# Remainders of the first layer's memory weights: made by adding DMAs onto the negated weights

## The chip, the cores and the metric

The kernel runs on one core of a Trainium2 chip. The metric is device time in microseconds for one execution of the whole program; the median of the runs is quoted. A profiled execution gives the durations used below.

## What is computed

A two-layer encoder over 512 tokens of width 1024. Each layer runs a token mixer (latent attention in the first layer, grouped-query attention in the second) beside a 4-head cross-attention into 256 memory tokens, merges both in one output projection, and then applies a SwiGLU block. The part that the change touches is the projection of the memory tokens into keys and values:

```python
def _memory_attention(q, mem_n, w_kv, q_norm, k_norm):
    q = _rmsnorm(q.reshape(B, S, MEM_HEADS, MEM_HEAD_DIM), q_norm)
    kv = (mem_n @ w_kv).reshape(B, M, 2, MEM_HEADS, MEM_HEAD_DIM)
    k = _rmsnorm(kv[:, :, 0], k_norm)
    v = kv[:, :, 1]
    s = jnp.einsum('bqhd,bmhd->bhqm', q, k)
    p = jax.nn.softmax(s * (MEM_HEAD_DIM ** -0.5), axis=-1)
    return jnp.einsum('bhqm,bmhd->bqhd', p, v).reshape(B, S, MEM_W)

mem_n = _rmsnorm(mem, mem_norm)
for i in range(DEPTH):
    ...
    mem_out = _memory_attention(q_mem, mem_n, w_mem_kv[i], memq_norm[i], memk_norm[i])
```

`w_kv` is 1024 x 1024 for each layer, so `mem_n @ w_kv` is 256 x 1024 x 1024.

## The kernel before

Every matrix product is taken in three passes (`mm3`, L137 to L139). Each fp32 operand is split into a leading part `hi`, its value rounded to the matmul's fp32r format, and a remainder `lo`, the value less `hi`, rounded the same way. The product is hi\*hi, hi\*lo and lo\*hi, summed in PSUM. A weight chunk goes through `load_w`: SyncE loads it from HBM into a tile `raw` (L170), ScalarE casts it into `whi` (L158), and VectorE subtracts to get `wlo` (L159).

The memory part (`mem_part`) of a layer is two halves, keys (c = 0) and values (c = 1), of eight chunks of 128 x 512 each: 16 chunks per layer. Each chunk is multiplied with two blocks of 128 memory tokens, so six matmuls of 512 columns per chunk; the first, third, fourth and sixth of them need only `whi`, the second and fifth need `wlo`. The PSUM banks of the first layer are named `mm_173` and `mm_174` (keys) and, for the values, `mm_264` and `mm_265`. The memory tokens themselves (`memT`) are scaled by gains into `g` tiles by ScalarE (L247) and VectorE (L250), and squared on ScalarE (L261).

In the first layer the memory part is one of four streams that `merge` writes out interleaved: attention units, the projections of queries and keys by head group (banks `sc`, later `mm`), the memory stages, and the start of the output projection. From what is written, the framework's scheduler fixes the order on each engine, with latencies of its own for each operation. Each engine then runs its list strictly in order, and waits on semaphores where a tile is not ready. POOL (GpSimd) issues a few loads of rotary tables at the start and then nothing until the first feed-forward block, where it issues DMAs that add a weight block in HBM onto a block in SBUF (L815, L947, L981). All other loads are issued by SyncE.

The weight pool holds 7 `raw`, 6 `whi` and 6 `wlo` tiles at this stage. A tile is reused once its readers are done.

Of the kernel before, what the change touches and what calls it, by code (L numbers as in the profile page):

```python
# [12 lines left out]
F32R = mybir.dt.float32r  # L13
I32 = mybir.dt.int32
AF = mybir.ActivationFunctionType
ALU = mybir.AluOpType
# [32 lines left out]
def encoder_kernel(ctx: ExitStack, tc: tile.TileContext, a: dict, out: bass.AP):  # L49
    nc = tc.nc  # L50
    V, A, PE, GP = nc.vector, nc.scalar, nc.tensor, nc.gpsimd
# [12 lines left out]
    def wtile(dt, tag, bufs=None):  # L64
        return wpool[0][1].tile([P, wpool[0][2]], dt, tag=tag, name=nm(tag), **({"bufs": bufs} if bufs else {}))
# [6 lines left out]
    def nm(s):  # L72
        uid[0] += 1
        return f"{s}_{uid[0]}"

    def g4(shape=(P, 1024), dt=F32R, name="g"):
        return gp_.tile(list(shape), dt, tag="G", name=nm(name))

    def pair(dt=F32R, n=512, name="g"):

        t = g4((P, 2, 512), dt, name)
        return t[:, 0, :n], t[:, 1, :n]
# [3 lines left out]
    def gt(shape=(P, 512), dt=F32R, kind=""):  # L86

        h = halves.pop((dt, kind), None)
        if h is None:
            h, halves[dt, kind] = pair(dt)  # L90
        if len(shape) == 2:
            return h[:, : shape[1]]
        if len(shape) == 3:
            return h.rearrange("p (a b) -> p a b", a=shape[1])
        return h.rearrange("p (a b c) -> p a b c", a=shape[1], b=shape[2])
# [7 lines left out]
    def bank(tag):  # L103
        return ps.tile([P, 512], F32, tag=tag, name=nm(tag), bufs=CFG[tag])
# [4 lines left out]
    def f(ap):  # L109
        return ap.bitcast(F32)  # L110
# [20 lines left out]
    def gcol(i):  # L131
        return gains[:, i : i + 1]


    def mm3(out, lh, rh, start, stop, skip=False):
        (lhi, llo), (rhi, rlo) = lh, rh
        PE.matmul(out, lhi, rhi, start=start, stop=False, skip_group_check=skip)  # L137
        PE.matmul(out, lhi, rlo, start=False, stop=False, skip_group_check=skip)  # L138
        PE.matmul(out, llo, rhi, start=False, stop=stop, skip_group_check=skip)  # L139
# [3 lines left out]
    def eng(kind):  # L143
        c = cnt.get(kind, 0)
        cnt[kind] = c + 1
        p = CFG[kind]
        return p[c % len(p)]

    phase = ["s"]

    def wsplit(raw, n, kind, neg=False):

        hi, lo = wtile(F32R, "whi"), wtile(F32R, "wlo")
        if neg:
            A.mul(hi[:, :n], raw, -1.0)
            V.scalar_tensor_tensor(lo[:, :n], raw, -1.0, f(hi[:, :n]), ALU.mult, ALU.subtract)
            return hi, lo
        A.copy(hi[:, :n], raw)  # L158
        (V if eng(kind) == "V" else GP).tensor_sub(lo[:, :n], raw, f(hi[:, :n]))  # L159
        return hi, lo  # L160
# [3 lines left out]
    def load_raw(src, n):  # L164
        if wpool[0][2] == 1024:
            nraw[0] += 1
            raw = wtile(F32, "raw", CFG["RF"]) if nraw[0] % 2 and CFG["RF"] else g4(dt=F32, name="raw")
        else:
            raw = wtile(F32, "raw", CFG["W"])
        nc.sync.dma_start(raw[:, :n], src)  # L170
        return raw

    def load_w(src, n):
        return wsplit(load_raw(src, n)[:, :n], n, "wlo" + phase[0])

    def w_units(src, unit):

        n = src.shape[1] // unit
        per = max(1, wpool[0][2] // unit)
        nch = -(-n // per)  # L180
        u = 0
        for c in range(nch):
            m = (n - u + nch - c - 1) // (nch - c)
            w = load_w(src[:, u * unit : (u + m) * unit], m * unit)
            for j in range(m):
                yield wcols(w, j * unit, (j + 1) * unit)
            u += m

    def wcols(w, a0, a1):
        return w[0][:, a0:a1], w[1][:, a0:a1]  # L190
# [54 lines left out]
    def split_gain(dst, src, g):  # L245
        if eng("hi") == "A":
            A.mul(dst[0], src, g)  # L247
        else:
            V.tensor_scalar_mul(dst[0], src, g)
        V.scalar_tensor_tensor(dst[1], src, g, f(dst[0]), ALU.mult, ALU.subtract)  # L250
# [5 lines left out]
    def acc_sq(acc, src, first):  # L256
        if first:
            A.activation(acc, src, AF.Square)
        else:
            s = tt()  # L260
            A.activation(s[:, : acc.shape[1]], src, AF.Square)  # L261
            V.tensor_add(acc, acc, s[:, : acc.shape[1]])
# [60 lines left out]
    def tsl(x, t):  # L323
        return x[0][:, t * P : (t + 1) * P], x[1][:, t * P : (t + 1) * P]
# [11 lines left out]
    def k_outer(outs, acts, src, ncols, tags, pre=()):  # L336

        outs += [bank(tg)[:, :ncols] for tg in tags]
        nk = len(acts)
        rest = w_units(src[:, len(pre) * ncols :], ncols)  # L340
        for k in range(nk):
            w = pre[k] if k < len(pre) else next(rest)
            for t in range(4):
                mm3(outs[t], tsl(acts[k], t), w, k == 0, k == nk - 1)
            yield 12 * ncols / 2370
# [247 lines left out]
    def mem_part(l, c, outs, hm):  # L593

        outs += [bank("mm"), bank("mm")]
        m = None
        per = CFG["WC"] // NM
        for k, w in enumerate(w_units(a["w_mkv"][l, c], 512)):
            if c == 0:
                if k % per == 0:  # L600
                    n = min(per, NK - k) * NM
                    m = load_raw(a["memT"][:, k * NM : k * NM + n], n)
                h = gt((P, 2, NM), kind="m")
                h = (h[:, 0], h[:, 1])
                split_gain(h, m[:, (k % per) * NM : (k % per + 1) * NM], gcol(G_MEM + k))
                hm.append(h)
                if l == 0:
                    if k == 0:
                        acc_m.append(gt(dt=F32)[:, :NM])
                    acc_sq(acc_m[0], m[:, (k % per) * NM : (k % per + 1) * NM], k == 0)  # L610
            h = hm[k]
            for t in range(2):
                mm3(outs[t], tsl(h, t), w, k == 0, k == NK - 1)
            yield 1.3

    def mem_stages(l, kts, vts):
        xs, ssqs, hm = [], [], []

        def k_head():
            outs = []  # L620
            yield from mem_part(l, 0, outs, hm)
            xs.extend(raw_copy(o, 512) for o in outs)
            ssq = small(8, "ssqm")
            for t in range(2):
                head_ssq(ssq[:, 4 * t : 4 * t + 4], [xs[t]], 4, P)
            ssqs.append(ssq)
# [21 lines left out]
        def v_head():  # L648
            outs = []
            yield from mem_part(l, 1, outs, hm)  # L650
            for t in range(2):
                v = pair()
                split_gain(v, outs[t], r_mem[0][:, t : t + 1])
                vts.append(v)
# [12 lines left out]
    def out_prefix(l, acts, banks, pre, n, tag, ready):  # L667


        while not ready():  # L670
            yield None
        banks += [bank(tag) for _ in range(n)]
        for kp in range(3):
            yield from out_block(banks, range(n), acts, kp, list(w_units(a["w_out"][l, 0, kp], 512)), kp == 0, False)
        pre.append(w_early(a["w_out"][l, 0, 3], 2))
        while (l, 7) not in fin:
            yield None
        weight_pool(True)
        pre.append(list(w_units(a["w_out"][l, 0, 4], 512)))
# [436 lines left out]
    for o in range(5):  # L1116
        c = pair()
# [475 lines left out]
```

## Time and profile before

| what | us |
|---|---|
| median of 3 runs | 1249.2 |
| lowest and highest run | 1248.47, 1249.56 |
| the profiled execution's own time | 1250.35 |
| its span, first to last instruction | 1248.2 |
| TensorE busy in the span | 1234.2 (99%) |
| VectorE busy | 996.7 (80%) |
| ScalarE busy | 754.4 (60%) |
| POOL busy | 63.5 (5%) |

The profiled execution took 1.15 us more than the median. Its span leaves out 2.15 us around the first and the last instruction. A matmul of 512 columns is shown with some 380 to 400 ns, but the next one starts about 227 ns after it: matmuls overlap in the array, so gaps under about 0.15 us between two of them don't show as idle time and are seen only in their starts.

### The profile page before, as it was taken

To read this page: it belongs to the slowest core of one execution; us is meant where nothing else is said; L and a number is where in the kernel's file an instruction comes from. 1 tells how busy PE (TensorE), PEld (TensorE's weight loads), DVE (VectorE), ACT (ScalarE), POOL (GpSimd) and SP (SyncE) were. 2 spreads that over 40 slices of the span, in tenths; PEclk is the share of its full clock that TensorE was granted. 3 is DMA by queue.
4 is the path that set the end of the run, shared out by engine and by line. 5 is a ranking of instruction groups with operands and counts; after the bars stand their busy time and mean duration, and the time that the engine had idled before them with its cause. 6 is when DMAs were issued, how large, how long until landed. Compare 5 with 4: busy or idle time off the path is not lost.

```text
span 1248.2 us, 17265 instructions
## 1 busy us (share of the span) xinstructions
PE 1234.2 (99%) x6305; PEld 1037.6 (83%) x6305; DVE 996.7 (80%) x1778; ACT 754.4 (60%) x1293; POOL 63.5 (5%) x83
## 2 busy tenths in 40 slices
PE   9999999999999999999999999999999999999998
PEld 6988878888778888888888888888887888889887
DVE  6699999854888877899857797976388977789984
ACT  6597776754755555577453578867375555556742
POOL 1000000001000000021100000000000000002110
PEclk9999999999999999999999999999999999999999
DMA  7342101055274344695733211323436344459681
GB/s 235 118 149 81 35 9 68 1 202 167 56 216 118 112 132 112 220 244 156 156 110 101 86 51 60 110 69 119 143 77 194 100 140 140 119 171 253 158 178 67
DMA packets 54964, 157.05 MB, mean 126 GB/s; under 512 B 6320, under 2 KB 10928, under 8 KB 54880
## 3 DMA queue, kind: packets, MB, share of 16 engines
q1 hardware_dynamic: 44784, 119.58, 27.7%
q0 software_dynamic: 10096, 36.38, 15.4%
q8 instruction: 49, 0.80, 0.3%
q14 instruction: 35, 0.29, 0.1%
HBM read 153.84 MB, written 2.10 MB: 125 GB/s over the span
## 4 chain that ended last, share of the span: by engine, by line
PE 94%; DVE 3%; ACT 2%; DMA 1%; issue 0%; SPq 0%
PE mm L138 15%; PE mm L139 14%; PE mm L137 14%; PE sc L138 12%; PE sc L137 12%; PE sc L139 12%; PE tp L351 6%; PE sc L504 4%; DVE wlo L159 1%; PE tp L137 1%; PE tp L139 1%; PE tp L138 1%; ACT whi L158 1%; PE tp L570 1%; DMA raw<-in_w_cin 1%; ACT t L902 0%
## 5 line engine op out<-in xcount | busy, mean ns | idle before, releaser
L158 ACT CAST whi<-raw 128x1024 fp32r<-128x1024 f32 (+3 forms) x370 | 330.5, 898 | 310.9 <-PE sc L139 199.9
L159 DVE TENSOR_TENSOR wlo<-raw,whi 128x1024 fp32r<-128x1024 f32 (+3 forms) x370 | 378.6, 1028 | 156.6 <-ACT whi L158 153.7
L138 PE MATMUL mm<-wlo,op 128*128 128x512 f32 (+1 forms) x456 | 172.7, 379 | 3.3 <-DVE wlo L159 3.3
L137 PE MATMUL mm<-whi,op 128*128 128x512 f32 (+1 forms) x456 | 173.0, 379 | 0.3 <-ACT whi L158 0.2
L139 PE MATMUL mm<-whi,op 128*128 128x512 f32 (+1 forms) x456 | 171.9, 377 | 0.0
L139 PE MATMUL sc<-whi,op 128*128 128x512 f32 (+1 forms) x456 | 171.6, 376 | 0.0
L138 PE MATMUL sc<-wlo,op 128*128 128x512 f32 (+1 forms) x456 | 171.6, 376 | 0.0
L137 PE MATMUL sc<-whi,op 128*128 128x512 f32 (+1 forms) x456 | 171.5, 376 | 0.0
L137 PE MATMUL mm<-whi,g 128*128 128x512 f32 (+3 forms) x370 | 141.3, 383 | 0.0
L138 PE MATMUL mm<-wlo,g 128*128 128x512 f32 (+3 forms) x370 | 139.1, 376 | 0.0
L139 PE MATMUL mm<-whi,g 128*128 128x512 f32 (+3 forms) x370 | 138.2, 376 | 0.0
L138 PEld LDWEIGHTS mm<-wlo,op 128*128 128x128 f32 x456 | 85.9, 188 | 20.9 <-DVE wlo L159 5.9
L137 PEld LDWEIGHTS mm<-whi,op 128*128 128x128 f32 x456 | 85.9, 188 | 15.9 <-ACT whi L158 0.8
L138 PEld LDWEIGHTS sc<-wlo,op 128*128 128x128 f32 x456 | 85.8, 188 | 15.7
L139 PEld LDWEIGHTS sc<-whi,op 128*128 128x128 f32 x456 | 85.8, 188 | 15.6
L137 PEld LDWEIGHTS sc<-whi,op 128*128 128x128 f32 x456 | 85.8, 188 | 15.5
L139 PEld LDWEIGHTS mm<-whi,op 128*128 128x128 f32 x456 | 85.9, 188 | 15.3
L137 PEld LDWEIGHTS mm<-whi,g 128*128 128x128 f32 x370 | 69.6, 188 | 10.5 <-ACT g L247 0.7
L139 PEld LDWEIGHTS mm<-whi,g 128*128 128x128 f32 x370 | 69.4, 188 | 10.5 <-DVE g L250 0.2
L138 PEld LDWEIGHTS mm<-wlo,g 128*128 128x128 f32 x370 | 69.7, 188 | 9.4
L504 PE MATMUL sc<-g,g 128*128 128x512 f32 x256 | 74.7, 411 | 0.6 <-ACT g L247 0.6
L815 POOL DMA_DIRECT2D raw<-in_w_gu x24 | 20.7, 863 | 882.3 <-DMA raw<-in_w_gu 544.6
(289 smaller groups left out, 2260.1 us busy)
## 6 DMA issues: line engine op xcount, KB each, us to landing
raw<-in_w_gu SPq DMA_DIRECT2D x80, 512.0 KB, 4.4
raw<-in_w_dn SPq DMA_DIRECT2D x44, 512.0 KB, 5.7
raw<-in_w_dn POOLq DMA_DIRECT2D x40, 512.0 KB, 10.6
raw<-in_w_gu POOLq DMA_DIRECT2D x24, 512.0 KB, 5.4
raw<-in_w_out SPq DMA_DIRECT2D x22, 512.0 KB, 4.9
raw<-in_w_mkv SPq DMA_DIRECT2D x32, 256.0 KB, 2.7
raw<-in_w_gin SPq DMA_DIRECT2D x30, 256.0 KB, 2.9
raw<-in_w_gl SPq DMA_DIRECT2D x8, 512.0 KB, 4.0
```

What stands on the lines that cost most here:

```text
L137: PE.matmul(out, lhi, rhi, start=start, stop=False, skip_group_check=skip)
L138: PE.matmul(out, lhi, rlo, start=False, stop=False, skip_group_check=skip)
L139: PE.matmul(out, llo, rhi, start=False, stop=stop, skip_group_check=skip)
L158: A.copy(hi[:, :n], raw)
L159: (V if eng(kind) == "V" else GP).tensor_sub(lo[:, :n], raw, f(hi[:, :n]))
L351: PE.transpose(dst[:, i * P : (i + 1) * P], s, ident)
L504: PE.matmul(sc, lq[:, q * P : (q + 1) * P], rk, start=i == 0, stop=i == len(passes) - 1)
L570: PE.transpose(tb4[:, k, j, :], self.p[j][:, k * P : (k + 1) * P], ident)
L815: GP.dma_start(raws[g, q][i], w_src(g, by)[i], accum_op=ALU.add)
```

## The change

For the 16 chunks of the first layer's memory weights alone, `load_w` is replaced by `wsplit_dma`. ScalarE casts as before. Where VectorE subtracted, ScalarE now multiplies the raw chunk by -1 into the `wlo` tile, which gives the negative of the leading part, and a DMA from POOL's queue adds the raw chunk, read once more from HBM, onto that tile. The second layer's memory weights and all other weights are split as before.

```diff
-    def load_w(src, n):
-        return wsplit(load_raw(src, n)[:, :n], n, "wlo" + phase[0])
-
-    def w_units(src, unit):
+    def wsplit_dma(raw, src, n):
+        hi, lo = wtile(F32R, "whi"), wtile(F32R, "wlo")
+        A.copy(hi[:, :n], raw)
+        A.mul(lo[:, :n], raw, -1.0)
+        GP.dma_start(lo[:, :n], src.bitcast(F32R), accum_op=ALU.add)
+        return hi, lo
+
+    def load_w(src, n, dma=False):
+        raw = load_raw(src, n)[:, :n]
+        return wsplit_dma(raw, src, n) if dma else wsplit(raw, n, "wlo" + phase[0])
+
+    def w_units(src, unit, dma=False):
...
-            w = load_w(src[:, u * unit : (u + m) * unit], m * unit)
+            w = load_w(src[:, u * unit : (u + m) * unit], m * unit, dma)
...
-        for k, w in enumerate(w_units(a["w_mkv"][l, c], 512)):
+        for k, w in enumerate(w_units(a["w_mkv"][l, c], 512, l == 0)):
```

In the program VectorE loses 16 instructions, ScalarE gains 16, and POOL gains 16 DMAs, which stand between its table loads and the first feed-forward block's adding DMAs. SyncE's list is the same. On TensorE, VectorE and ScalarE the scheduler orders the first layer's mixer anew, up to the output projection; from there on the lists are as before. In the listings the number behind a name's first underscore is the buffer, which is the same in both programs; later numbers differ by a few. In the changed kernel L177 is the cast, L178 the negation and L179 the adding DMA.

First place, TensorE at the third chunk of the keys (`whi_203`, `wlo_204`), with `sc_208` a bank of the query projection. Before:

```order
L137 MATMUL mm_173_821<-whi_203_910,g_206_916 128x512
L138 MATMUL mm_173_821<-wlo_204_911,g_206_916 128x512
L137 MATMUL mm_174_822<-whi_203_910,g_206_916 128x512
L139 MATMUL mm_173_821<-whi_203_910,g_206_916 128x512
L138 MATMUL mm_174_822<-wlo_204_911,g_206_916 128x512
L139 MATMUL mm_174_822<-whi_203_910,g_206_916 128x512
L137 MATMUL sc_208_928<-whi_189_876,g_90_418 128x384
```

And now:

```order
L137 MATMUL mm_173_821<-whi_203_912,g_206_919 128x512
L137 MATMUL mm_174_822<-whi_203_912,g_206_919 128x512
L137 MATMUL sc_208_931<-whi_189_878,g_90_418 128x384
L138 MATMUL sc_208_931<-wlo_190_879,g_90_418 128x384
L139 MATMUL sc_208_931<-whi_189_878,g_90_418 128x384
L137 MATMUL sc_208_931<-whi_192_884,g_91_422 128x384
L138 MATMUL sc_208_931<-wlo_193_885,g_91_422 128x384
L139 MATMUL sc_208_931<-whi_192_884,g_91_422 128x384
L137 MATMUL sc_208_931<-whi_195_890,g_93_428 128x384
L138 MATMUL sc_208_931<-wlo_196_891,g_93_428 128x384
L138 MATMUL mm_173_821<-wlo_204_913,g_206_919 128x512
```

The two matmuls that need only `whi_203` stay at their place; eight matmuls of 384 columns now stand ahead of the first that needs `wlo_204`.

Second place, ScalarE around the first chunk of the values (`whi_267`, `wlo_268`); `sc_258` is a bank that TensorE fills just ahead of that chunk, `mm_173` and `mm_174` are the finished keys. Before, the cast of `whi_267` stands nine rows ahead of these:

```order
L158 CAST whi_281_1205<-raw_280_1203 128x512
L409 COPY t_259_1121<-mm_173_821 128x512
L241 ACTIVATE sqw_262_1126<-t_259_1121 128x512
L409 COPY t_260_1123<-mm_174_822 128x512
L1256 COPY t_247_1072<-sc_258_1111 128x256
L247 ACTIVATE g_250_1082<-sc_258_1111,rc_98_444 128x256
L241 ACTIVATE sqw_263_1129<-t_260_1123 128x512
L158 CAST whi_290_1244<-raw_289_1242 128x512
```

And now:

```order
L177 CAST whi_267_1144<-raw_266_1142 128x512
L419 COPY t_259_1129<-mm_173_821 128x512
L419 COPY t_260_1131<-mm_174_822 128x512
L251 ACTIVATE sqw_262_1134<-t_259_1129 128x512
L1266 COPY t_247_1079<-sc_258_1119 128x256
L257 ACTIVATE g_250_1089<-sc_258_1119,rc_98_444 128x256
L251 ACTIVATE sqw_263_1137<-t_260_1131 128x512
L178 ACTIVATE wlo_268_1145<-raw_266_1142 128x512
L1266 COPY t_248_1080<-sc_274_1176 128x256
```

The cast has moved down to the copies of the keys, and the negation of this chunk comes seven rows after it, behind copies that wait for TensorE to fill `mm_174` and `sc_258`.

Third place, TensorE ahead of the same chunk's first use of `wlo_268`, now (before, `wlo_268` was the second matmul after `sc_258` was full). Two matmuls with `whi_267` and the six of bank `sc_274` come between `sc_258` and these rows; `t_198` is query rows that VectorE scales (L435 before) and TensorE then transposes into `tp_283` and `tp_285`:

```order
L137 MATMUL sc_279_1203<-whi_241_1068,g_95_434 128x512
L138 MATMUL sc_279_1203<-wlo_242_1069,g_95_434 128x512
L139 MATMUL sc_279_1203<-whi_241_1068,g_95_434 128x512
L137 MATMUL sc_279_1203<-whi_244_1074,g_96_438 128x512
L138 MATMUL sc_279_1203<-wlo_245_1075,g_96_438 128x512
L139 MATMUL sc_279_1203<-whi_244_1074,g_96_438 128x512
L361 MATMUL tp_283_1229<-ident_88,t_198_895 128x128 x2
L361 MATMUL tp_285_1237<-ident_88,t_198_895 128x128 x2
L138 MATMUL mm_264_1140<-wlo_268_1145,g_179_832 128x512
```

Before, one matmul stood between the filled `sc_258` and the first use of `wlo_268`; now fourteen matmuls of 512 columns and four transposes do.

## Rows read from the trace of the kernel before

**Rows 1.** Page, part 1: busy us, share of the span, instructions of each engine.

```profile
PE 1234.2 (99%) x6305; PEld 1037.6 (83%) x6305; DVE 996.7 (80%) x1778; ACT 754.4 (60%) x1293; POOL 63.5 (5%) x83
```

**Rows 2.** Page, part 4: shares of the chain that ended last, by engine.

```profile
PE 94%; DVE 3%; ACT 2%; DMA 1%; issue 0%; SPq 0%
```

**Rows 3.** Stretches of the first layer's mixer: length, busy us of each engine, clock, DMA.

```profile
core 0: us, PE busy (x) PEld busy (x) DVE busy (x) ACT busy (x) POOL busy (x), PEclk, DMA share, GB/s
40.00:64.00 24.00, 24.00 (x188) 24.00 (x187) 14.34 (x60) 11.53 (x29) 0.00 (x0) 1.00 0.35 109
64.00:85.00 21.00, 21.00 (x105) 17.70 (x104) 19.13 (x40) 19.51 (x47) 0.00 (x0) 1.00 0.48 153
85.00:95.00 10.00, 10.00 (x51) 8.48 (x49) 9.90 (x28) 8.82 (x19) 0.00 (x0) 1.00 0.41 135
95.00:110.00 15.00, 14.79 (x77) 12.24 (x76) 14.84 (x55) 8.94 (x21) 0.00 (x0) 1.00 0.39 118
```

**Rows 4.** Timelines: the first and last remainder, the first chunk on TensorE, POOL's next DMA.

```profile
48.12 0.69 DVE L159 TENSOR_TENSOR wlo<-raw,whi 128x512 fp32r<-128x512 f32 x1 [1.07 <-ACT whi L158]
64.83 0.50 PE L137 MATMUL mm<-whi,g 128*128 128x512 f32 x1
101.46 0.69 DVE L159 TENSOR_TENSOR wlo<-raw,whi 128x512 fp32r<-128x512 f32 x1
294.42 0.90 POOL L815 DMA_DIRECT2D raw<-in_w_gu  x1 [287.83 <-DMA raw<-in_w_gu]
```

**Rows 5.** Groups by shape, 40 to 110 us: busy us, mean ns | idle before, releaser.

```profile
L159 DVE TENSOR_TENSOR wlo<-raw,whi 128x512 fp32r<-128x512 f32 x24 | 16.3, 687 | 4.2 <-ACT whi L158 4.2
L158 ACT CAST whi<-raw 128x512 fp32r<-128x512 f32 x24 | 14.7, 621 | 7.3 <-PE sc L139 3.9 <-PE mm L139 3.0
L247 ACT ACTIVATE g<-tp,gains 128x512 fp32r<-128x512 f32 x7 | 4.7, 698 | 0.0
```

**Rows 6.** Waits of TensorE's weight loads, 94 to 110 us: total, times, longest.

```profile
PEld tp L266 <- DVE g L1273: 0.4, 1, 0.4
PEld sc L504 <- ACT g L247: 0.3, 1, 0.3
PEld tp L351 <- PE tp L351: 0.3, 1, 0.3
PEld tp L351 <- DVE t L1237: 0.3, 1, 0.3
```

**Rows 7.** Timeline of TensorE at three places: start, us, instruction.

```profile
68.23 0.40 PE L137 MATMUL mm<-whi,g 128*128 128x512 f32 x1
68.46 0.39 PE L138 MATMUL mm<-wlo,g 128*128 128x512 f32 x1
...
69.61 0.34 PE L137 MATMUL sc<-whi,g 128*128 128x384 f32 x1
69.79 0.35 PE L138 MATMUL sc<-wlo,g 128*128 128x384 f32 x1
...
85.03 0.39 PE L137 MATMUL mm<-whi,g 128*128 128x512 f32 x1
85.26 0.39 PE L138 MATMUL mm<-wlo,g 128*128 128x512 f32 x1
...
96.65 0.63 PE L351 MATMUL tp<-ident,t 128*128 128x128 f32 x4
```

**Rows 8.** Timeline of ScalarE: start, us, instruction, count.

```profile
65.94 1.21 ACT L158 CAST whi<-raw 128x512 fp32r<-128x512 f32 x2
...
85.27 0.38 ACT L1256 COPY t<-sc 128x256 f32<-128x256 f32 x1
85.53 0.49 ACT L247 ACTIVATE g<-sc,rc 128x256 fp32r<-128x256 f32 x1
85.90 0.64 ACT L241 ACTIVATE sqw<-t 128x512 f32<-128x512 f32 x1
86.42 1.03 ACT L158 CAST whi<-raw 128x512 fp32r<-128x512 f32 x2
...
96.40 0.59 ACT L1272 CAST g<-tp 128x512 fp32r<-128x512 f32 x1 [1.49 <-PE tp L351]
```

**Rows 9.** Timeline of VectorE ahead of the first transposes of query rows.

```profile
87.26 0.69 DVE L159 TENSOR_TENSOR wlo<-raw,whi 128x512 fp32r<-128x512 f32 x1
...
90.42 1.89 DVE L435 TENSOR_TENSOR t<-t,hs 128x512 f32<-128x512 f32 x3
```

**Rows 10.** DMA issues of the whole run: engine, count, KB each, median us to landing.

```profile
raw<-in_w_gu SPq DMA_DIRECT2D x80, 512.0 KB, 4.4
raw<-in_w_dn POOLq DMA_DIRECT2D x40, 512.0 KB, 10.6
raw<-in_w_gu POOLq DMA_DIRECT2D x24, 512.0 KB, 5.4
raw<-in_w_mkv SPq DMA_DIRECT2D x32, 256.0 KB, 2.7
g<-in_rope_gqa POOLq DMA_DIRECT2D x2, 256.0 KB, 4.6
```

**Rows 11.** The adding DMAs of line L815: landing times of all 26.

```profile
DMA to landing us min/median/max: 5.1/5.4/8.6
```

## The prediction

> **What bounds the kernel now.** I read the shares of the engines first. TensorE is busy 99% of the span [rows 1], and 94% of the chain that ended last is TensorE [rows 2]. A time can fall only where TensorE waits, and it rises wherever an edit makes TensorE wait. So the next view is the table of stretches around the edited work, whose first and last remainders are made at 48 and 101 us [rows 4]. Three things are to be seen in it [rows 3]. TensorE has no idle time from 40 to 95 us and 0.21 us from 95 to 110. VectorE is close to full from 85 to 110 us (24.74 of 25). ScalarE is close to full from 64 to 95 us (28.33 of 31) and has room behind that. The clock is granted in full throughout. So the work moves between two engines that are nearly full, beside a third that never waits; what counts is whether the remainder still arrives before TensorE asks for it.
>
> **What VectorE gets back.** It loses 16 subtractions of 0.687 us [rows 5], 11.0 us. TensorE can gain no more than it waits for VectorE there. From 64 to 94 us it waits for next to nothing; from 94 to 110 us its weight loads wait 0.4 us and 0.3 us directly for VectorE and 0.3 us for a transpose that is itself late [rows 6], and 0.21 us is plain idle time [rows 3]. Together that is 1.0 to 1.2 us. By 95 us VectorE has shed 12 subtractions, so I take all of it as gained: -1.2 us. If the new order kept those waits, it would be 0.
>
> **What ScalarE takes on.** 16 negations of 128x512. The nearest rows are the cast with 0.621 us and the scaling by a gain with 0.698 us [rows 5]; the negation is of the second kind, so 0.70 us and 11.2 us in all. Two of them fall ahead of 64 us, where ScalarE is half idle (11.53 of 24) and the first chunk is not begun before 64.83 us [rows 4]; they cost nothing. About 11 fall between 64 and 95 us, 7.7 us into 2.7 us of idle time [rows 3]. What of that is on TensorE's path is in the sums below, since each negation there is placed by the order; the rest runs over into the idle time behind 95 us (6.06 us up to 110).
>
> **What the DMA costs.** POOL has nothing else to do from its table loads to 294 us [rows 4], so no queue stands ahead of the 16 DMAs and none behind them is reached. The 4.2 MB that they read again come on top of DMA engines that are 39 to 48% busy [rows 3]; the loads that they might slow land several microseconds before their cast. What counts is L, the time from issue on POOL to landing. The trace has no adding DMA of 256 KB. Adding DMAs of 512 KB land in 5.4 us (5.1 to 8.6) at line L815 [rows 10, 11] and in 10.6 us where several were queued behind one another. Plain loads from POOL of 256 KB land in 4.6 us, plain loads by SyncE of 256 KB in 2.7 and of 512 KB in 4.4 us [rows 10], so halving the size saves about 1.7 us. 5.4 - 1.7 = 3.7 us for an undisturbed add; here loads run beside it, as with the 4.6 us. I take L = 4.2 us, between these two and nearest to both; the ends are 2.7 us (a plain hardware load) and 5.4 us (the add of twice the size).
>
> The rule that would bring the time out elsewhere stands in the Trainium skill, DMA: Bandwidth & Descriptors, section on the anatomy of one DMA on the GpSimd path: about 2.0 us fixed plus bytes over 436 GB/s. For 256 KB that is an estimate of 2.6 us, at which the sum below would be near zero; for 512 KB it gives 3.2 us, where the trace has 5.4 [rows 10], so the trace doesn't agree for adds.
>
> **Three places where TensorE would stand still.** The new order answers the longer chain by moving the matmuls that need a remainder back. I walk each place with the starts of the trace: a matmul of 512 columns every 0.23 us, of 384 every 0.18 us, a transpose every 0.12 us [rows 7].
>
> Place one, the third chunk (`wlo_204`). Its cast starts at 65.94 us as the first of two in a row [rows 8]; the negation takes the second one's place at 66.5, ends at 67.2, and the sum is there at 67.3 + L. TensorE begins the chunk at 68.23 and, after two matmuls of 512 and eight of 384, wants the remainder at 68.23 + 0.46 + 1.44 = 70.1. Wait: L - 2.8, that is 1.4 us.
>
> Place two, the ninth chunk (`wlo_268`). The negation now stands behind the copies of `sc_258` and the squares, where a cast stands at 86.42 [rows 8]: it ends at 87.1, and the sum is there at 87.2 + L. TensorE is at the chunk at 85.03, and after fourteen matmuls and four transposes at 85.03 + 3.22 + 0.48 = 88.7. Wait: L - 1.5, that is 2.7 us. Part of that shows ahead of the remainder, at the transposes into `tp_283`: VectorE scaled their input from 90.42 us on [rows 9]; with one subtraction less just ahead (0.69 at 87.26) that is about 89.8, and TensorE gets there at 88.25. So this place costs 1.55 us even with a fast DMA.
>
> Place three, the 13th chunk (`wlo_309`). On ScalarE the negation follows the cast of a transposed bank (`tp_287`), as the row at 96.40 shows one, freed by the transposes [rows 8]. Counted from the last of these transposes: 0.27 us to its end, 0.59 + 0.70 us on ScalarE less 0.1 for their overlap, so the sum lands after about 1.6 + L. In that time TensorE has three matmuls of 512, four transposes, eight of 384, two of 512, the column sums (0.2 at most) and five of 384: 0.69 + 0.48 + 1.44 + 0.46 + 0.2 + 0.9, and 0.12 for the transpose itself, 4.3 us. Wait: L - 2.7, that is 1.5 us.
>
> The other 13 chunks keep a cover of L or a little less; where the order leaves under half a microsecond (fourth, sixth and eighth) I add 0.5 us in all, 0.2 with a short L and 1.0 with a long one.
>
> **Sum.** 1.4 + 2.7 + 1.5 + 0.5 - 1.2 = +4.9 us, rounded to 4.8. Nothing behind takes it back: TensorE stays the bound to the end and every later load hangs on tiles that TensorE frees. On the profiled execution, 1250.35 us with 2.15 us around its span, that gives 1255.15; that execution lies 1.15 us over the median, so the forecast of the median is 1249.2 + 4.8 = 1254.0 us.
>
> **Rivals.**
> The landing is quick. At L = 2.7 us, the row of SyncE's loads of the same weights [rows 10], places one and three are covered and place two costs its 1.55: 0 + 1.55 + 0 + 0.2 - 1.2 = +0.55, 1249.8 us. Against it speaks that no DMA from POOL in these rows lands under 4.6. The skill's figure above comes to the same. Everything up to L = 3.5, about +2.5 us, reads as no change. 20%.
> VectorE was the hidden brake. If its 11.0 us set the pace from 85 to 110 us, TensorE would get its 1.2 us and, with place two gone as VectorE's scaling comes early by the whole 6 us shed up to there, some matmul starts that slid by under 0.15 us each without showing as idle; with some ten of these, 1.5 us more. That is -2.7, 1246.5 us. It decides once L stays under about 2.8. TensorE's unbroken 31.00 of 31 us from 64 to 95 [rows 3] speaks against it. 5%.
> The sum is late. Adds that met loads took up to 8.6 us, and 10.6 where they stood in a queue [rows 10, 11]. Chunks here come some 3 us apart, so at L above 3 two are in flight at times. At 7.3 us the three places cost 4.5 + 5.8 + 4.6, and five more chunks about 1 us each lose their cover: +18.7, 1268 us. 8%.
> ScalarE becomes the bound. If all of the 5.0 us that don't fit in its idle time held up TensorE and the DMA hardly anything, the result would be 5.0 - 1.2 = +3.8, 1253.0 us, with waits for banks that ScalarE empties in place of waits for DMAs. The idle time behind 95 us speaks against it. 12%.
>
> **How the numbers follow.** The forecast has 55%, the rivals 20, 5, 8 and 12%. The range: at the low end L near 2.7 with most of VectorE's gain, 1249.5; at the high end L = 5.4 gives 2.6 + 3.9 + 2.7 + 1.0 - 1.2 = +9.0, and one more place at 2 us, 1260.5. Below the range lie VectorE's case and some of the quick landings, above it the late sums. A measurement of this kernel tells about 0.2%, 2.5 us, from no change: faster 5%, within 20%, slower 75%.
>
> **What would show it.** In the changed profile: landings of POOL's adds from `in_w_mkv` with a median of 3.7 to 4.6 us; TensorE's waits naming that DMA, three long ones (1 to 3 us) near 70, 90 and 100 us; ScalarE over 90% busy from 64 to 100 us, VectorE down to some 75%; every stretch behind 280 us as long as before. The prediction is wrong if the adds land in under 3.3 us, if the long waits name ScalarE's copies, or if TensorE's waits there sum to under 3 us.

## The result and the profile after

The changed kernel takes 1263.8 us in the median of four runs (1262.3 to 1264.7), beside 1249.4 us (1248.5 to 1250.5) for the kernel before on the same chip: a ratio of 1.0111, with a 95% interval of 1.0099 to 1.0123, or 14.4 us more. The forecast was 1254.0 us and the range ended at 1260.5. The sign was right; the loss is three times as large as forecast.

The profiled execution of the changed kernel took 1264.44 us, its span is 1262.6 us, 14.4 us longer than the one of before. The page's first part, then its chain by engine and its groups of DMA issues (count, KB each, median us to landing), answer to [rows 1, 2, 10]:

```profile
PE 1237.2 (98%) x6305; PEld 1039.3 (82%) x6305; DVE 989.4 (78%) x1762; ACT 761.8 (60%) x1309; POOL 77.3 (6%) x99
...
PE 91%; issue 2%; ACT 2%; DVE 2%; DMA 2%; SPq 0%; POOL 0%; POOLq 0%
...
raw<-in_w_mkv SPq DMA_DIRECT2D x32, 256.0 KB, 2.9
...
wlo<-in_w_mkv POOLq DMA_DIRECT2D x16, 256.0 KB, 5.5
```

VectorE has lost its 16 instructions (x1778 to x1762) and 7 us of busy time, ScalarE has gained 16 and 7 us, and the span grew by 14.4 us. The adds land in 5.5 us in the median, not 4.2. The stretches of the mixer (columns as in [rows 3]) show where the time went, and the last row here and the two rows of before behind it where some of it came back:

```profile
64.00:85.00 21.00, 18.75 (x88) 16.13 (x87) 10.21 (x21) 16.97 (x41) 5.14 (x6) 0.92 0.70 163
85.00:95.00 10.00, 7.74 (x33) 5.69 (x32) 7.09 (x22) 7.53 (x18) 0.17 (x1) 1.00 0.45 113
95.00:110.00 15.00, 9.02 (x44) 6.35 (x43) 9.04 (x21) 9.14 (x20) 3.28 (x4) 1.00 0.80 188
110.00:125.00 15.00, 12.89 (x61) 11.48 (x60) 11.07 (x53) 8.44 (x21) 3.45 (x4) 0.89 0.68 144
125.00:200.00 75.00, 74.00 (x440) 63.65 (x439) 72.61 (x191) 59.55 (x136) 0.00 (x0) 1.00 0.11 34
```

The same view of the kernel before, 64 to 125 us and 125 to 200 us:

```profile
64.00:125.00 61.00, 60.59 (x311) 50.47 (x310) 58.69 (x163) 49.86 (x114) 0.00 (x0) 1.00 0.37 116
125.00:200.00 75.00, 72.52 (x422) 61.43 (x421) 70.67 (x193) 55.92 (x129) 0.00 (x0) 0.98 0.06 18
```

From 64 to 125 us TensorE is idle for 2.25 + 2.26 + 5.98 + 2.11 = 12.6 us where it was idle for 0.4. No other engine is full there any more: VectorE, which had 24.74 of 25 us from 85 to 110 [rows 3], now has 16.1, and ScalarE 16.7. From 64 to 125 us ScalarE's waits name TensorE (17 of 19 us) and VectorE's name ScalarE: they idle because TensorE is late. The loads beside the adds land later too (`w_kvb` in 4.5 us in the median, 2.8 before), but no wait of TensorE or ScalarE in this stretch names a load. The waits of TensorE (in total, times, longest) from 40 to 130 us say for what:

```profile
PE mm L138 <- DMA wlo<-in_w_mkv: 11.6, 8, 2.4
PE tp L361 <- DVE t L445: 1.0, 1, 1.0
```

Eight waits name the adding DMA. Here are the timelines of POOL, with the eight issues of these adds, and of TensorE, with the matmuls that waited for them and one group of transposes (start, duration, in brackets the idle time ahead and its releaser):

```profile
68.06 0.86 POOL L179 DMA_DIRECT2D wlo<-in_w_mkv  x1 [12.80 <-ACT wlo L178]
...
81.10 0.86 POOL L179 DMA_DIRECT2D wlo<-in_w_mkv  x1 [3.13 <-ACT t L271]
83.93 0.86 POOL L179 DMA_DIRECT2D wlo<-in_w_mkv  x1 [1.97 <-PE tp L361]
94.83 0.87 POOL L179 DMA_DIRECT2D wlo<-in_w_mkv  x1 [10.04 <-ACT wlo L178]
96.56 0.86 POOL L179 DMA_DIRECT2D wlo<-in_w_mkv  x1 [0.87 <-ACT t L1266]
98.24 0.86 POOL L179 DMA_DIRECT2D wlo<-in_w_mkv  x1 [0.82 <-ACT wlo L178]
99.28 0.86 POOL L179 DMA_DIRECT2D wlo<-in_w_mkv  x1 [0.17 <-issue]
110.40 0.87 POOL L179 DMA_DIRECT2D wlo<-in_w_mkv  x1 [10.26 <-ACT wlo L178]
...
73.17 0.50 PE L138 MATMUL mm<-wlo,g 128*128 128x512 f32 x1 [2.25 <-DMA wlo<-in_w_mkv]
...
88.01 0.50 PE L138 MATMUL mm<-wlo,g 128*128 128x512 f32 x1 [1.66 <-DMA wlo<-in_w_mkv]
...
90.28 0.50 PE L138 MATMUL mm<-wlo,g 128*128 128x512 f32 x1 [0.60 <-DMA wlo<-in_w_mkv]
...
96.82 0.66 PE L361 MATMUL tp<-ident,t 128*128 128x128 f32 x4 [1.02 <-DVE t L445]
98.99 0.50 PE L138 MATMUL mm<-wlo,g 128*128 128x512 f32 x1 [1.51 <-DMA wlo<-in_w_mkv]
...
101.43 0.50 PE L138 MATMUL mm<-wlo,g 128*128 128x512 f32 x1 [0.46 <-DMA wlo<-in_w_mkv]
...
105.78 0.50 PE L138 MATMUL mm<-wlo,g 128*128 128x512 f32 x1 [2.40 <-DMA wlo<-in_w_mkv]
...
107.78 0.50 PE L138 MATMUL mm<-wlo,g 128*128 128x512 f32 x1 [0.59 <-DMA wlo<-in_w_mkv]
...
115.36 0.79 PE L138 MATMUL mm<-wlo,g 128*128 128x512 f32 x1 [2.11 <-DMA wlo<-in_w_mkv]
```

Since TensorE starts within some 0.05 us of the landing, a pair of rows gives one add's own time: 73.17 - 68.06 = 5.1 us for the third chunk, 88.01 - 81.10 = 6.9 for the seventh, 6.4 for the eighth, 98.99 - 94.83 = 4.2 for the ninth, 4.9 for the tenth, 7.5 for the eleventh, 8.5 for the twelfth, 5.0 for the 13th. These are no scatter: in a second profiled execution (e11 below) the same chunks have 5.0, 6.7, 6.1, 4.2, 6.7, 7.3, 8.1 and 4.7; only the tenth differs by more than half a microsecond.

The clock adds to it. Two stretches of TensorE, some 3.4 us each, ran at the lower level, 1.2 GHz, in the granted clock (next to last columns: clock, DMA share, GB/s):

```profile
70.00:72.00 2.00, 0.92 (x6) 0.60 (x4) 1.22 (x3) 2.00 (x5) 0.85 (x1) 1.00 0.85 171
72.00:74.00 2.00, 0.83 (x4) 0.70 (x5) 0.00 (x0) 0.20 (x1) 0.86 (x1) 1.00 0.85 185
...
74.00:77.40 3.40, 3.40 (x12) 3.10 (x11) 0.62 (x2) 2.38 (x6) 0.28 (x1) 0.51 1.01 252
115.40:118.40 3.00, 3.00 (x8) 2.61 (x9) 1.07 (x3) 1.14 (x2) 0.43 (x1) 0.50 1.02 216
```

TensorE had been idle for 2.25 us of the four before the first, and for 2.11 us just before the second. Each costs up to half its length, 1.7 us, together 3.4 us. Not every long wait has such a stretch behind it: after the longest, the 2.40 us up to 105.78, the clock stays at 1.00.

**The sum of the difference.** Idle time 64 to 125 us: 12.6 - 0.4 = +12.2. A wait shown as 2.25 us delays the next start by 2.41, since matmuls overlap; over the nine waits the starts are 1.5 us later than the idle time tells (14.1 against 12.6): +1.5. Half clock in the mixer: +3.4. From 125 to 200 us the kernel before was idle for 2.48 us and lost 1.7 us to a stretch at half clock near 188 us; the changed kernel is idle for 1.00 us at full clock: -3.2. From 200 us on TensorE is idle for 0.6 us more in 1000: +0.6. That makes +14.5 of the 14.4 us.

### The profile page after: what moved, and what is told of

Same layout as the page of the kernel before. It is cut to its first block, busy times and chain, and to the rows that moved or that the text cites. A ratio compares the mean times of both kernels' runs of the same rounds, so it can differ in the third digit from the quotient of the medians.

```text
span 1262.6 us, 17307 instructions
## 1 busy us (share of the span) xinstructions
PE 1237.2 (98%) x6305; PEld 1039.3 (82%) x6305; DVE 989.4 (78%) x1762; ACT 761.8 (60%) x1309; POOL 77.3 (6%) x99
## 4 chain that ended last, share of the span: by engine, by line
PE 91%; issue 2%; ACT 2%; DVE 2%; DMA 2%; SPq 0%; POOL 0%; POOLq 0%
PE mm L138 14%; PE mm L139 14%; PE mm L137 14%; PE sc L137 12%; PE sc L138 12%; PE sc L139 12%; PE tp L361 5%; PE sc L514 5%; DMA wlo<-in_w_mkv 1%; PE tp L139 1%; PE tp L138 1%; PE tp L137 1%; DVE wlo L159 1%; ACT whi L158 1%; PE tp L580 1%
## 5 line engine op out<-in xcount | busy, mean ns | idle before, releaser
L158 ACT CAST whi<-raw 128x1024 fp32r<-128x1024 f32 (+3 forms) x354 | 320.7, 910 | 310.1 <-PE sc L139 201.8
L159 DVE TENSOR_TENSOR wlo<-raw,whi 128x1024 fp32r<-128x1024 f32 (+3 forms) x354 | 367.1, 1042 | 158.5 <-ACT whi L158 155.4
L138 PE MATMUL mm<-wlo,g 128*128 128x512 f32 (+3 forms) x370 | 140.8, 380 | 11.6 <-DMA wlo<-in_w_mkv 11.6
```

## Experiments

All start from the changed kernel; each is compared with the kernel before on the same chip.

**e1: the negation without the DMA.** What does ScalarE's new work cost by itself, with the sum on VectorE again?

```diff
-        GP.dma_start(lo[:, :n], src.bitcast(F32R), accum_op=ALU.add)
+        V.tensor_add(lo[:, :n], raw, f(lo[:, :n]))
```

> The negation stays on ScalarE for the 16 chunks, but VectorE adds the raw chunk to it; no DMA adds. Theory A (the sums come late by DMA): no waits of TensorE on a DMA there, no stretch of half clock in the first layer's mixer before 130 us, +2 to +3 us against the kernel before, 1251 to 1253, since ScalarE has 11 us more to do and VectorE nothing less. Theory B (ScalarE became the bound): most of the 14.4 us stays, 1259 or more.

Measured: 1253.2 against 1249.95 us, ratio 1.0027 (1.0017 to 1.0037), +3.3 us, just above what theory A gave. TensorE's waits from 40 to 130 us, and its stretch from 64 to 125:

```profile
PE tp L361 <- DVE t L1247: 1.0, 1, 1.0
PE mm L138 <- DVE wlo L179: 0.8, 2, 0.5
PE tp L361 <- DVE g L260: 0.3, 1, 0.3
...
64.00:125.00 61.00, 58.80 (x292) 47.91 (x291) 56.94 (x152) 53.47 (x122) 0.00 (x0) 1.00 0.35 112
```

TensorE is idle for 2.2 us there, with VectorE's 16 instructions kept and ScalarE's 16 added. So some 11 of the 14.4 us come with the DMA. This is no exact share: the scheduler gives this kernel an order of its own, so its 3.3 us can't simply be taken off the changed kernel's loss.

**e4: a quicker landing, everything else the same.** The add reads the raw chunk from its tile in SBUF instead of from HBM.

```diff
-        GP.dma_start(lo[:, :n], src.bitcast(F32R), accum_op=ALU.add)
+        GP.dma_start(lo[:, :n], raw.bitcast(F32R), accum_op=ALU.add)
```

> As the changed kernel, but the DMA adds the raw chunk from its tile in SBUF, not from HBM a second time. If the read from HBM makes the adds slow, they land in 4 us or less and the time falls to 1254 or below. If the add itself (read, add and write of the tile by the DMA engines, 16 engines shared with the loads) sets it, they land in 5 to 6 us as before and the time stays at 1261 to 1265.

Measured: 1255.6 against 1249.95 us, ratio 1.0038 (1.0023 to 1.0053), +5.7 us. TensorE, VectorE and ScalarE run the same lists in the same order as in the changed kernel, so the adds' source and their landing (min, median, max) are what differs, and with it the waits and the clock:

```profile
DMA to landing us min/median/max: 3.2/4.0/5.9
...
PE mm L138 <- DMA wlo<-raw: 5.7, 8, 1.6
...
64.00:125.00 61.00, 54.17 (x264) 43.51 (x263) 45.60 (x128) 49.61 (x112) 12.00 (x14) 1.00 0.70 172
```

The changed kernel has 4.1, 5.5 and 8.5 us in the first of these rows. With 1.5 us less of landing 5.9 us of waits on sums are gone and so are both stretches at half clock; the loss falls from 14.4 to 5.7 us. The landing is the lever. It is at the 4 us that the first case named, but the time is 1.6 us above that case's bound. Note the eight waits that remain at a median of 4.0 us; the comparison below comes back to them.

**e8: the negation on VectorE.** This frees ScalarE, and the DMA stays.

```diff
-        A.mul(lo[:, :n], raw, -1.0)
+        V.tensor_scalar_mul(lo[:, :n], raw, -1.0)
```

> The negation is made by VectorE instead of ScalarE (one operand instead of two, into the same tile); the adding DMA from HBM and its place stay. ScalarE is freed of the 16 extra instructions. If the loss comes from TensorE's waits for late sums (landings of 5 to 6 us against a cover of about 4), it stays: +8 to +13 us over the kernel before, about 1258 to 1263 us, with 8 to 13 us of TensorE's waits naming the adding DMA and landings with a median of 5 to 6 us. If ScalarE's load were what delays the chain (its rival), the loss falls to about +3 us, 1253 us, with under 4 us of waits on that DMA.

Measured: 1258.7 against 1249.8 us, ratio 1.0074 (1.0059 to 1.0089), +9.0 us. Landings (min, median, max) and TensorE's waits on sums from 40 to 130 us:

```profile
DMA to landing us min/median/max: 4.1/5.9/8.2
...
PE mm L138 <- DMA wlo<-in_w_mkv: 6.7, 4, 2.3
```

The landings are as long as in the changed kernel; the waits on sums are below the 8 us expected at least. Without any of ScalarE's 16 instructions the loss is still 9 us, so ScalarE isn't the bound. It is part of the chain, though: on VectorE several negations come earlier, their chunks have more cover (5.4 us instead of 2.7 for the third, 9.1 instead of 2.5 for the ninth), and four waits are left of eight.

**e10: fewer bytes.** Only the first 128 of each chunk's 512 columns are added.

```diff
-        GP.dma_start(lo[:, :n], src.bitcast(F32R), accum_op=ALU.add)
+        GP.dma_start(lo[:, : n // 4], src[:, : n // 4].bitcast(F32R), accum_op=ALU.add)
```

> The adding DMA adds the first 128 of each chunk's 512 columns only; the other 384 columns of the remainder stay at the negated weights, so that part of the computation is left out. Each add moves 64 KB instead of 256 KB; ScalarE's work, the queue and the order are nearly those of the changed kernel. If the landing is mostly the bytes and the loads beside them, landings fall to 2.5 to 3.5 us, TensorE's waits on these DMAs under 3 us, and the loss to between 0.5 and 4 us, 1250 to 1254 us. If the landing is mostly a fixed cost of a DMA from POOL, it stays above 3.5 us and the loss above 5 us.

Measured: 1254.1 against 1250.2 us, ratio 1.0031 (1.0019 to 1.0042), +3.9 us. The same two rows of this kernel:

```profile
DMA to landing us min/median/max: 2.7/3.6/5.0
...
PE mm L138 <- DMA wlo<-in_w_mkv: 4.3, 5, 1.5
```

The loss is at the edge of the first case, landings and waits are a little above what it gave: a quarter of the bytes takes 1.9 us off the median, and 3.6 us remain. So neither case holds alone. Most of a landing doesn't go with the bytes, but what does go with them decides about ten of the 14 us. Not all of the ten need be the bytes, since the scheduler's order in the mixer differs in places from the changed kernel's.

**e2 and e3: keys alone, values alone.**

```diff
-        for k, w in enumerate(w_units(a["w_mkv"][l, c], 512, l == 0)):
+        for k, w in enumerate(w_units(a["w_mkv"][l, c], 512, l == 0 and c == 0)):
```

(`c == 1` for the values.)

> Adding DMAs for the eight chunks of the keys alone, the values are subtracted by VectorE. Theory A: TensorE waits for DMAs at three of the eight key chunks, 4.5 to 5.5 us in all as in the changed kernel (2.4 + 1.8 + 0.8), with one stretch of half clock worth 1.7 us: +5 to +8 us, 1254 to 1257. Theory B: half of the negations, about +7, but with the waits on ScalarE's tiles.

> Adding DMAs for the eight chunks of the values alone. Theory A: the five waits at the values' chunks stay, 8 us in the changed kernel (1.7 + 0.6 + 2.7 + 0.8 + 2.3), less where the order differs, and one stretch of half clock: +5 to +9 us, 1254 to 1258. With the keys' run it should sum to about the 14.4 us of the whole change. Theory B: as many us as the keys, about +7.

Measured, both against 1249.95 us: keys 1257.7, ratio 1.0052 (1.0037 to 1.0067), +7.8 us; values 1259.0, ratio 1.0062 (1.0043 to 1.0082), +9.1 us. Landings have medians of 5.6 and 5.2 us, and TensorE waits 4.0 us (three times) and 5.6 us (three times) for sums. Neither half is the culprit. The halves add up to 16.8 us, more than both together: in e3 TensorE's wait of 1.9 us for VectorE near 190 us stands as before and two stretches at half clock lie in the mixer and one behind it, so what the changed kernel gets back later, this one doesn't. And not all of e2's loss is late sums: its waits of TensorE from 40 to 130 us also hold a long one for ScalarE, just ahead of 128 us, with a second stretch at half clock behind it:

```profile
PE sc L514 <- ACT g L257: 1.8, 1, 1.8
```

e6 has the same wait with 1.4 us. The changed kernel has none there, so theory B holds for a part of e2, but not for the change.

**e6: every second chunk.** Are the landings long because adds queue behind one another?

```diff
-            w = load_w(src[:, u * unit : (u + m) * unit], m * unit, dma)
+            w = load_w(src[:, u * unit : (u + m) * unit], m * unit, dma and c % 2 == 1)
```

> As the changed kernel, but only every second chunk of each half goes by the adding DMA, so that two adds are seldom in flight together. If adds slow one another, they land in a median of 4.0 to 5.0 us, against 5.5, and the loss falls by more than half, to 1253 to 1256. If only the loads slow them, they land in 5.5 us as before and the loss is about half of 14.4 us, 1256 to 1258.

Measured: 1257.9 against 1250.25 us, ratio 1.0060 (1.0045 to 1.0074), +7.6 us. The same two rows:

```profile
DMA to landing us min/median/max: 4.1/5.1/6.3
...
PE mm L138 <- DMA wlo<-in_w_mkv: 5.7, 4, 2.3
```

Three pairs of its eight adds still overlap, by 1.1, 0.2 and 1.8 us, and the median is 5.1 us; what is gone is the tail, 6.3 instead of 8.5 us at most. The loss is what the second case gave. The changed kernel's own adds say the same: the five issued while no other was in flight landed in 4.1 to 5.1 us, the eleven issued while one was in flight in 4.6 to 8.5, median 6.3 (in e11: 4.2 to 5.0, and 5.0 to 8.1). So adds in a row go with the longest landings, not with the usual 5 us.

**e5 and e7: written three chunks ahead.** The chunks' loads, negations and adds are written out up to three chunks before the matmuls that use them, with the add from HBM (e5) or from SBUF (e7).

```diff
-            w = load_w(src[:, u * unit : (u + m) * unit], m * unit, dma)
-            for j in range(m):
-                yield wcols(w, j * unit, (j + 1) * unit)
+            spans.append((u, m))
...
+        for c, (u, m) in enumerate(spans):
+            for u2, m2 in spans[len(ws) : c + 1 + (3 if dma else 0)]:
+                ws.append(load_w(src[:, u2 * unit : (u2 + m2) * unit], m2 * unit, dma))
+            for j in range(m):
+                yield wcols(ws[c], j * unit, (j + 1) * unit)
```

> As the changed kernel (adds read from HBM), but each chunk's load, cast, negation and add are written out three chunks ahead of its matmuls. Theory A (TensorE waits because the sum comes later than the order allows for): the waits on these DMAs fall from 12 us to 2 to 4 us, although the adds land no sooner (5 to 6 us), and the time falls to 1251 to 1255. Theory B (the cost is in ScalarE's 16 further instructions or in the DMA traffic): both are as large as before, 1261 to 1265.

> Both remedies: the add reads the chunk from SBUF (landing 4.0 us in the run with that alone) and everything is written three chunks ahead. Theory A: waits on the adds of 1 to 2 us in all, 1249 to 1252, and no stretch of half clock; if VectorE's 11 us were worth something beyond the waits of the kernel before, a little under 1249.9. Theory B: as the run with SBUF alone, 1255.

Measured, both against 1250.25 us: e5 1256.6, ratio 1.0047 (1.0031 to 1.0064), +6.4 us; e7 1254.1, ratio 1.0028 (1.0018 to 1.0038), +3.8 us. Landings in e5 are as long as in the changed kernel (4.4 to 7.8, median 6.0), but waits on sums fall from 11.6 to 4.5 us: cover works as well as speed. Both remedies together leave two waits for sums and 2.5 us in e7 (TensorE's waits, 40 to 130 us):

```profile
PE mm L138 <- DMA wlo<-raw: 2.5, 2, 1.3
PE tp L366 <- DVE g L265: 1.4, 1, 1.4
```

Still e7 is slower than the kernel before, and both runs are slower than theory A gave them, in part because this order brings a wait of 1.4 us for VectorE that the kernel before doesn't have. No version with all 16 adds came out at or below it.

**e9: the first two chunks alone.** They have 13 to 17 us between issue and first use, 9 to 12 us between landing and first use (the expectation below has the first distance under the second's name).

```diff
-            w = load_w(src[:, u * unit : (u + m) * unit], m * unit, dma)
+            w = load_w(src[:, u * unit : (u + m) * unit], m * unit, dma and c < 2)
...
-        for k, w in enumerate(w_units(a["w_mkv"][l, c], 512, l == 0)):
+        for k, w in enumerate(w_units(a["w_mkv"][l, c], 512, l == 0 and c == 0)):
```

> Only the first two chunks of the keys go by negation and adding DMA; the other 14 are subtracted on VectorE as before. In the changed kernel these two had 13 to 16 us between landing and first use. If the loss is a matter of cover, this run is within 0.2% of the kernel before (1247.5 to 1252.5 us), with no wait of TensorE on an adding DMA. If an adding DMA cost something wherever it stands (by its traffic, or by its effect on the loads beside it), two of sixteen would cost about 1.8 us and the loads of these weights would land later than 2.7 us.

Measured: 1250.4 against 1249.8 us, ratio 1.0006 (0.9996 to 1.0015), no difference that can be told. The adds land in 4.3 and 5.1 us, no wait of TensorE names them, and the loads of these weights land in 2.8 us (2.7 before). An add with cover costs nothing that can be told, and it gives nothing back either. Its profiled execution shows something else behind the stage, in TensorE's longest wait and in the stretch from 125 to 200 us:

```profile
PE tp L361 <- DVE t L445: 1.9, 1, 1.9
...
125.00:200.00 75.00, 72.52 (x432) 61.67 (x431) 72.25 (x198) 56.86 (x133) 0.00 (x0) 1.00 0.06 18
```

It is the wait of 1.9 us of the kernel before, with the same idle time (72.52 busy), but the clock stays at 1.00 where before had 0.98. The same wait was followed by half clock in one execution and not in the other.

**e11: the changed kernel once more.**

> The changed kernel once more. The waits for sums hang on the order and on landings of 4 to 8 us, so they should repeat: 10 to 13 us of TensorE's waits on the adding DMA between 64 and 125 us. The two stretches of 3.4 us at half clock, ahead of 77 and of 118 us, either repeat within some us (then they belong to these waits, and a loss of 12 to 15 us includes their 3.4 us), or they are elsewhere or missing (then the part of the loss put down to the clock is a matter of the single execution, and its time is lower by 1.7 us for each one that is missing).

Measured: 1263.2 against 1250.2 us, ratio 1.0107 (1.0092 to 1.0122), +13.0 us. TensorE's waits on sums from 40 to 130 us, and its stretch from 64 to 125:

```profile
PE mm L138 <- DMA wlo<-in_w_mkv: 11.2, 10, 2.1
...
64.00:125.00 61.00, 48.81 (x214) 38.65 (x212) 37.17 (x113) 40.67 (x93) 12.02 (x14) 0.92 0.68 156
```

The waits repeat (11.2 and 11.6 us). The stretches at half clock don't: here none follows the wait at 70 to 72 us, and there are three, one from about 98 us and two in a row from about 115 us. The sum stays; part of a stretch at half clock lies ahead of a wait for the next sum and only shortens it, which is the likely reason, not a measured one. The mean granted clock, which every run has, bears out that the cost comes along: it was 0.995 to 0.997 in all eight executions of the changed kernel on record, 0.998 to 1.000 in those of e4 and e10, and 0.997 to 1.000, mostly 0.998 or more, in those of the kernel before. Only the place of a stretch differs from one execution to the other.

## Why the prediction missed

**The bound and the sign: right.** TensorE is the bound, the edit made it wait, the waits name the adding DMA and not ScalarE's copies. None of the three signs that the prediction named for being wrong appeared; none of them was set against a loss much larger than the forecast. Of what it said would show it, though, three things failed: the landings have a median of 5.5 us and not of 3.7 to 4.6, eight waits name the DMA and not three, and ScalarE is busy for 24.5 of the 31 us from 64 to 95, not over 90%.

**The three places: right, but for the landing.** Measured from the starts, the next matmul was due 2.70 us after the issue at place one, 2.48 at place two and 2.70 at place three. The waits were 2.41, 1.18 + 1.67 = 2.85 and 2.27 us, 7.5 in all, where the prediction had 1.4, 2.7 and 1.5, 5.6 in all. Set the landings of these three adds (5.1, 4.2 and 5.0 us) into its own terms, L - 2.8, L - 1.5 and L - 2.7, and they give 2.3, 2.7 and 2.3. The negation's 0.64 us were right as well (0.70 taken); from its end to POOL's issue there are 0.29 us, where 0.1 was taken.

**The other 13 chunks: the step that failed.** "The other 13 chunks keep a cover of L or a little less", with 0.5 us for all of them. Five of them cost 1.83, 0.76, 0.62, 2.65 and 0.75 us, 6.6 in all. Their cover in the changed kernel was 5.1, 5.6, 4.2, 4.9 and 7.8 us, at or above the L = 4.2 taken, but their adds landed in 6.9, 6.3, 4.8, 7.5 and 8.5 us. One L stood for 16 adds of which no two have the same neighbours. And part of this cover was made by the waits ahead: in e4, where TensorE is less late, the covers of the fourth, fifth, eighth, eleventh and twelfth chunks are 3.5, 4.4, 3.6, 3.4 and 4.2 us, and at a median landing of 4.0 us these five still cost 0.61 + 0.96 + 1.19 + 0.61 + 1.72 = 5.1 us. So even with adds a little quicker than the 4.2 taken the term was ten times too small: the covers sit close to L, and then it is the spread of the landings that is paid.

**Why L was too short.** The working took the 512 KB adds at 5.4 us [rows 10, 11] and subtracted 1.7 us for half the size, the difference between plain loads of SyncE. The 256 KB adds take 5.5 us. In e10 a quarter of the bytes saves 1.9 us, in e4 reading from SBUF saves 1.5, and in e6 keeping most adds apart saves 0.4 of the median and 2.2 of the longest. The working also left out what an add takes of the DMA engines while it runs beside loads. This is the view of the DMA queues from 94 to 110 us of the changed kernel (packets, MB, share of 16 engines):

```profile
q0 software_dynamic: 576, 1.05, 40.2%
q1 hardware_dynamic: 1008, 1.77, 34.7%
```

Adds (q0) spent 0.402 x 16 x 16 us over 576 packets, 179 ns for 1.8 KB each; the loads (q1) 88 ns for about as many bytes. An add's packet takes twice as long. The trace of the kernel before had this already. These are its queues over the whole span; 34.6 of the 36.4 MB of q0 are adding DMAs:

```profile
q1 hardware_dynamic: 44784, 119.58, 27.7%
q0 software_dynamic: 10096, 36.38, 15.4%
```

That is 305 ns for 3.6 KB in q0 and 123 ns for 2.7 KB in q1, 1.8 times as much for each byte. The share of the DMA engines from 95 to 110 us rose from 0.39 [rows 3] to 0.80, with about 1 MB of adds. The rule that the prediction set beside its sum, in the Trainium skill, DMA: Bandwidth & Descriptors, section on the anatomy of one DMA on the GpSimd path, gives an estimate of 2.6 us for 256 KB and of 2.15 us for 64 KB; here they are 5.5 and 3.6 us, so it doesn't hold for adds beside loads, neither in size nor in slope. The difference between e4 and the changed kernel, 1.5 us, is not time of packets in the DMA engines: from 64 to 125 us an add's packet took 171 ns in e4 and 176 ns in the changed kernel. Whether it is HBM's answer under load or the adds' share of its bandwidth, no run here tells.

**The clock: not in the sum.** Half clock in the mixer costs 3.4 us. The prediction read "granted in full throughout" from the mixer's rows of before, where TensorE never waited; the kernel before shows what follows a wait elsewhere, near 188 us, and the prediction didn't look there.

**"Nothing behind takes it back": wrong.** Some 3 us come back between 125 and 200 us. There the kernel before waits 1.9 us for VectorE's scaling of query rows, and in this execution then runs at half clock. In the changed kernel the wait for these rows is gone, and one of 0.4 us for other query rows is new. This is the scheduler's new order and not TensorE's lateness: e4, with the lists of the changed kernel, has the same 0.4 us and no more although TensorE is some 9 us less late there, and e3, with the order of before in this place, keeps the 1.9 us although TensorE is 9 us late. VectorE's relief, -1.2 us in the sum, can't be seen apart. Most of the 1.2 were waits of weight loads, behind which TensorE stayed busy; idle time to be gained ahead of 125 us was 0.4 us, it is gone among the waits for sums, and no run separates the rest.

**In all.** The loss is 14.4 where 4.8 was forecast (the terms give 4.9), 9.6 us more: 1.9 at the three places, 6.1 at the others, 3.4 for the clock, about 0.8 of VectorE's 1.2 that didn't come, less 2.6 regained behind. The rival of late sums had the mechanism nearer than the forecast: it named landings up to 8.6 us and lost cover on five more chunks, at a price of 18.7 us, but with an L of 7.3 for all, where the three places had 4.1 to 5.1. ScalarE as the bound fell with e8, the quick landing with the first row of landings; VectorE as the hidden brake asked for an L under about 2.8 us, which no kernel with all 16 adds had.

## What to carry to other kernels

Before work is moved from an engine to a DMA, list the cover of every tile, from issue to first use, and hold it against the slowest landing rather than the median: with covers of 2.5 to 8 us and landings of 4 to 8.5 us half of 16 tiles made TensorE wait, while two tiles with 13 us of cover or more cost nothing that can be told. Beside an engine that is 99% busy, no run showed a gain from relieving its neighbour of 16 instructions; each microsecond of new latency on a tile with no slack was paid in full, and the clock charged extra. Where an adding DMA is used all the same, its source in SBUF landed 1.5 us sooner than the same bytes in HBM and issuing it several tiles ahead took most of the waits away.

## What the runs showed of the hardware

- Adding DMAs of 256 KB landed in 4.1 to 8.5 us, median 5.5, from HBM (the changed kernel; median 6.2 in e11) and in 3.2 to 5.9, median 4.0, from SBUF (e4); of 64 KB from HBM in 2.7 to 5.0, median 3.6 (e10). In the changed kernel those that were issued with no other add in flight took 4.1 to 5.1 us. POOL took 0.86 us in the median to issue one, in all three kernels.
- A packet of such an add took 179 ns, a load's packet of nearly the same size 88 ns, in the same 16 us of the changed kernel.
- In the middle of dense work, waits of 1.4 us (e6, near 128 us) to 2.4 us were followed by some 3.4 us at the lower clock, in some executions and places and not in others: near 115 us in both executions of the changed kernel, near 74 us in one of them, not after its longest wait near 105 us, and after the same wait near 184 us in the kernel before but not in e9. e4 and e10, whose longest waits are 1.6 and 1.5 us, show none.
